# A retention and state space mixer: its state recurrences placed among the projections, its output transposes one chunk later, and the first attention worked by pairs of heads

## The chip, the cores and the metric

The kernel runs on one core of a Trainium2 chip. The core has TensorE (PE, with its weight loads PEld), VectorE (DVE), ScalarE (ACT), GpSimd (POOL) and SyncE (SP, which issues most DMAs). The metric is the device time of one execution in microseconds (us), given as the median of the runs.

## What is computed

The reference is a small network of two blocks. The first takes 512 tokens of width 1024 through a projection, an attention of 8 heads of 64 dimensions that mixes three dilation patterns, a spatial gating, a layer norm and a mixture of 32 experts. The second block treats 512 latent tokens and a context of 256 tokens, in two layers. The first layer mixes by retention and a state space model, the second by latent-compressed attention, each followed by a gated feed-forward part. The mixer of the first layer is what most of this change is about:

```python
def chunked_decay_scan(q, k, v, log_a, s0):
    ...
    scores = jnp.einsum('bhnid,bhnjd->bhnij', qc, kc) * decay
    y_intra = jnp.einsum('bhnij,bhnjv->bhniv', scores, vc)
    ...
    kv_chunk = jnp.einsum('bhnjd,bhnj,bhnjv->bhndv', kc, to_end, vc)
    def step(s, inp):
        kv_n, tot_n = inp
        return tot_n[..., None, None] * s + kv_n, s
    ...
    y_inter = jnp.einsum('bhnid,bhni,bhndv->bhniv', qc, jnp.exp(cum), s_before)
```

It runs forwards and backwards, for 8 retention heads (q, k, v from the projection, q and k of the latents with rotary embedding, a fixed decay per head) and for 8 state space heads (SSD: a convolved input, a decay that depends on the token). The context starts from zero, and the latents start from the context's last states. Then both results are normalised, multiplied by gates, put side by side and multiplied by an output matrix.

## The kernel before

All large products are taken in float32 by splitting each operand into two halves of fp32r, high and low (`split`, L239 and L240: ACT copies the high half `wh`, DVE subtracts for the low half `wl`), and by three matmuls (`mm3`). A projection, `gemm_a`, goes over chunks of 512 output columns; a chunk's weights are four casts of 128x1024, and for each of the token tiles (four for the latents) 24 matmuls of 128x512 into a bank `ga` follow, and an evacuation. A scheduler puts the emitted instructions in order on each engine from the order in which they are written and from what they need; generators with `yield` let two pieces of code be written interleaved.

**First attention** (`block1`). For each head, four score products (queries of tile qt against the keys of tiles 0 to qt, K of 64 rows, into a bank `sc`), on DVE the mask's add, the row maximum, and after ACT's exponential one reciprocal of 128x4 for the head and a multiplication. Then the probabilities `pr` are transposed by PE (`tpb`) and copied to `pt`; at every second head the two heads' value products go to `pvb`, in the two column halves of the array. `fill(FL[3])` steps a filler three times a head: matmuls with one column of weights (`adb`) for the second block's modulation.

**The latent mixer** (`lm`, a class `Mixer` with `proj`, `rope`, `spread`, `states`, `outputs`). The trace has it from 762.5 to 1004.3 us. It is written in this order: the q and k projections with the SSD's time steps among them (`steps`: `smp`, `dt`, a chain of small DVE instructions, `expb`); `rope` of q and of k; the v projection; `spread`, which transposes x, q and k (`mtb`); `states`, which for each of four chunks of 128 tokens forms the retention's products (`kv_ret`: DVE scales v into `vfb`, PE gives `kvr`, DVE and ACT copy it to `SBr`), then for each the SSD's (`kv_ssd`: `btb`, `xsd`, `kvsb`, `SBs`), and then runs the recurrence over the chunks both ways (`carry`: on POOL for the retention, L1240 and L1241, on DVE for the SSD, L1243 and L1244). `outputs` then goes over the chunks n: `inside(n)` (retention scores `ret_s` and `PT`; the SSD's decay matrix `ssd_x` with `Rf` and `Rb` from `mask`, its exponential `E`, `ssd_s`; then the part of the states, `ret_i` with `rint` and `ssd_i` with `sint`), and one chunk behind it `gather(n-1)` (`ret_o` and `ssd_o`, the norms and gates, the result in `res`) and at once `turn(n-1)`, which transposes the result by PE (`ytb`, L1404) into `yT` for the output projection. That projection (`ga` from `yT`) follows, its first weights `wro` being loaded by `early` in the last chunk; then the norm for the next part (`ntb`).

The context's mixer (two chunks) runs the same code, stepped as filler among the experts of the first block.

```python
for n in range(self.nt + 1):
    if n < self.nt:
        o[n] = yield from self.inside(n)
        ...
    if n >= 1:
        self.gather(n - 1, o.pop(n - 1), ynw)
        if self.lat:
            self.turn(n - 1)
```

## Time and profile before

| | us |
|---|---|
| median of 3 runs | 2356.21 (2354.01 to 2359.71) |
| the profiled execution | 2353.49 |
| its span, first to last instruction | 2351.7 |
| PE busy | 2252.5 (96%) |
| DVE busy | 1423.6 (61%) |
| ACT busy | 794.9 (34%) |
| POOL busy | 442.9 (19%) |

A busy share is taken over the whole span, which holds stages with different limits: in the experts (some 300 to 640 us) the DMA engines are the busiest, in most of the rest PE. The mean granted clock of TensorE was 0.977 of full speed. A stage is read from its own stretch of the windows view, where the busy times of all engines and the granted clock stand side by side; what an engine stood idle for is read from the waits.

### The profile page before, as it was taken

How to read it: one execution, taken by the hardware profiler on the slowest of the kernel's cores; microseconds unless marked ns; L12 is line 12 of the kernel's file. 1: busy time of each engine (PE TensorE's matmuls, PEld its weight loads, DVE VectorE, ACT ScalarE, POOL GpSimd, SP SyncE). 2: the span in 40 equal slices, each digit the busy share in tenths (PEclk: the TensorE clock that was granted, in tenths of full speed). 3: DMA queues.
4: the chain of work that ended last, by engine and by line, in shares of the span. 5: the costliest groups of instructions: out<-in, count | busy, mean ns of one | idle time of the engine just before them, and what ended most of it. 6: DMA issues, size and time to landing. Idle time of an engine off the chain costs nothing.

```text
span 2351.7 us, 30149 instructions
## 1 busy us (share of the span) xinstructions
PE 2252.5 (96%) x11748; PEld 1688.6 (72%) x11748; DVE 1423.6 (61%) x2341; ACT 794.9 (34%) x1382; POOL 442.9 (19%) x331
## 2 busy tenths in 40 slices
PE   9999999999979988899999999989999999999998
PEld 7667755534458756688888888877877668888876
DVE  8766743434475577776677753465568765444446
ACT  4344323222253243342211112134446545222222
POOL 0010310232250256410000000531022123000006
PEclk9999999999989997999999999999999999999999
DMA  8655498998853001344344331221100043332230
GB/s 297 217 183 202 182 373 332 371 389 336 310 197 99 30 28 54 125 152 135 122 139 135 126 108 55 65 97 62 60 1 1 1 147 107 106 99 92 87 106 39
DMA packets 99151, 338.91 MB, mean 144 GB/s; under 512 B 14373, under 2 KB 16293, under 8 KB 99002
## 3 DMA queue, kind: packets, MB, share of 16 engines
q1 hardware_dynamic: 94394, 324.33, 39.1%
q0 software_dynamic: 4608, 12.59, 1.5%
q8 instruction: 94, 1.54, 0.3%
q14 instruction: 55, 0.45, 0.1%
HBM read 323.21 MB, written 17.86 MB: 145 GB/s over the span
## 4 chain that ended last, share of the span: by engine, by line
PE 72%; DVE 8%; issue 3%; POOL 2%; ACT 2%; DMA 0%; POOLq 0%; SPq 0%; DVEq 0%; ACTq 0%
PE gb L243 22%; PE ob L243 14%; PE ga L243 10%; PE cb L243 6%; PE gu L243 5%; PE sc L243 3%; PE yb L243 3%; PE ptb L1808 2%; DVE wl L240 1%; POOL rs_r L290 1%; PE kb L243 1%; PE vb L243 1%; PE ntb L920 1%; PE ssd_x L243 1%; PE tpm L687 1%
## 5 line engine op out<-in xcount | busy, mean ns | idle before, releaser
L239 ACT CAST wh<-wr 128x1024 fp32r<-128x1024 f32 (+1 forms) x239 | 249.1, 1048 | 629.1 <-PE gb L243 274.9
L240 DVE TENSOR_TENSOR wl<-wr,wh 128x1024 fp32r<-128x1024 f32 (+1 forms) x235 | 309.2, 1323 | 216.4 <-ACT wh L239 211.8
L243 PE MATMUL gb<-fh,wh 128*128 128x512 f32 x672 | 264.0, 393 | 0.0
L243 PE MATMUL gb<-fh,wl 128*128 128x512 f32 x672 | 263.9, 393 | 0.0
L243 PE MATMUL gb<-fl,wh 128*128 128x512 f32 x672 | 263.7, 392 | 0.0
L243 PE MATMUL ob<-wh,hidh 128*128 128x512 f32 x440 | 173.9, 395 | 4.4 <-DVE gob L1529 3.0
L243 PE MATMUL ob<-wl,hidh 128*128 128x512 f32 x440 | 172.5, 392 | 0.0
L243 PE MATMUL ob<-wh,hidl 128*128 128x512 f32 x440 | 172.3, 392 | 0.0
L1536 DVE TENSOR_TENSOR acc<-acc,ob 128x512 f32<-128x512 f32 x160 | 108.3, 685 | 84.6 <-PE ob L243 84.6
L860 DVE SCALAR_TENSOR_TENSOR adacc<-wr,cond,adacc 128x512 f32<-128x512 f32 x224 | 152.9, 752 | 1.4 <-DMA wr<-in_w_ada 1.4
L243 PEld LDWEIGHTS gb<-fh,wl 128*128 128x128 f32 x672 | 126.2, 188 | 28.7
L243 PEld LDWEIGHTS gb<-fl,wh 128*128 128x128 f32 x672 | 126.2, 188 | 27.7
L243 PEld LDWEIGHTS gb<-fh,wh 128*128 128x128 f32 x672 | 126.2, 188 | 27.4
L243 PE MATMUL gu<-mw,xgT 128*64 128x512 f32 x512 | 124.3, 600 | 0.7 <-issue 0.7
L243 PE MATMUL cb<-fh,wh 128*128 128x256 f32 x416 | 118.0, 284 | 0.0
L243 PE MATMUL cb<-fl,wh 128*128 128x256 f32 x416 | 117.6, 283 | 0.0
L243 PE MATMUL cb<-fh,wl 128*128 128x256 f32 x416 | 117.0, 281 | 0.0
L1538 POOL TENSOR_TENSOR acc<-acc,gate 128x1024 f32<-128x1024 f32 x10 | 28.1, 2811 | 468.1 <-DVE acc L1536 468.1
L290 POOL TENSOR_TENSOR rs_r<-rs_v,mhalf 128x1 f32<-128x1 f32 (+1 forms) x54 | 46.4, 861 | 336.8 <-DVE rs_v L288 336.5
L243 PEld LDWEIGHTS ob<-wh,hidh 128*128 128x128 f32 x440 | 82.6, 188 | 24.8 <-DVE gob L1529 3.2
L1491 DVE TENSOR_TENSOR sg<-sg,gb 128x512 f32<-128x512 f32 x42 | 28.9, 688 | 112.3 <-PE gb L243 112.2
L243 PEld LDWEIGHTS ob<-wh,hidl 128*128 128x128 f32 x440 | 82.7, 188 | 18.3
(666 smaller groups left out, 4891.3 us busy)
## 6 DMA issues: line engine op xcount, KB each, us to landing
mw<-in_w_gu SPq DMA_DIRECT2D x128, 512.0 KB
wr<-in_w_ada SPq DMA_DIRECT2D x96, 512.0 KB
mw<-in_w_dn SPq DMA_DIRECT2D x64, 512.0 KB
wr<-in_w_fg SPq DMA_DIRECT2D x44, 512.0 KB
wr<-in_w_fu SPq DMA_DIRECT2D x44, 512.0 KB
wr<-in_w_fd SPq DMA_DIRECT2D x44, 512.0 KB
wr<-in_w_ret SPq DMA_DIRECT2D x28, 512.0 KB
wr<-in_w_in SPq DMA_DIRECT2D x19, 512.0 KB
```

The costliest lines, as they stand in the source:

```text
L239: self.nc.scalar.copy(h, src)
L240: (eng or self.nc.vector).tensor_tensor(l, src, h.bitcast(F32), ALU.subtract)
L243: self.nc.tensor.matmul(out, lhsT, rhs, start=start, stop=stop, **kw)
L290: nc.gpsimd.tensor_tensor(r, v, self.mhalf[:, :n], ALU.pow)
L687: nc.tensor.transpose(bank[:, k, :], xg[:, (j * 4 + k) * P:(j * 4 + k + 1) * P], self.ident)
L860: V.scalar_tensor_tensor(acc[:, r], W[:, k], s, acc[:, r], op0=ALU.mult, op1=ALU.add)
L920: nc.tensor.transpose(bank[:, j, i * P:i * P + P], hp[i][:, (2 * kk + j) * P:(2 * kk + j + 1) * P], self.ident)
L1491: nc.vector.tensor_tensor(t, t, out[1], ALU.mult)
L1536: V.tensor_tensor(a[:, sl], a[:, sl], ob, ALU.add)
L1538: G.tensor_tensor(a, a, gate(tt), ALU.mult)
L1808: nc.tensor.transpose(bank[:, qt * P:qt * P + P], prs[h][qt][:, kt * P:kt * P + P], K.ident)
```

## The change

The first attention goes by pairs of heads p. For a tile of queries the two heads' score products are written one behind the other (they read the two halves of the rows of `qT` and `kT`), into banks of two tags, from the longest (qt = 3) to the shortest; each tile of queries has its own maximum, sum and reciprocal of 128x1; the odd head's probabilities lie in `res`. The transposes and value products of a pair are written among the scores of the next pair. The filler has the same number of steps as before.

In the mixer, `rope` is done tile by tile in the evacuation of q and k. `states` becomes `states_s` (SSD) and `states_r` (retention). The latents' `spread_x`, `kv_ssd` and SSD recurrence are written among the tiles of the q and k projections, at 1.25 steps a tile; `inside(0)` without `ret_i`, and then the retention's states, among the tiles of the v projection and behind it. `ret_i` moves into `carried(n)`, behind the states; the next chunk's mask is written behind it. The transposes `turn` come one chunk later. The loads of `wro` are written behind `outputs`. The tiles `xsd` and `sts` get large buffers of their own for the latents. The number of matmuls is the same.

```diff
-FL = (0, 1, 1, 3, 1)
+FL = (0, 1, 1, (2, 2, 1, 1), 1)
...
+        def scores(p, qt):
...
+            sc = [ps.tile([P, 512], F32, name="sc", tag=tag, bufs=2) for tag in ("sc", "mm")]
+            for c in range(2):
+                r = slice(64 * c, 64 * c + 64)
+                self.mm(sc[c][:, :n], qT[r, p, qt * P:qt * P + P], kT[r, p, :n], True, True)
+            for c in range(2):
...
+                V.tensor_tensor(pv, sc[c][:, :n], amask[:, 512 - n:], ALU.add)
+                V.tensor_reduce(mx, pv, AX, ALU.max, negate=True)
+                S.activation(pv, pv, AF.Exp, bias=mx, accum_out=ls)
+                V.reciprocal(ls, ls)
+                V.tensor_scalar(pv, pv, ls, None, op0=ALU.mult)
...
+        for p in range(5):
+
+            for i in range(NT):
+                if p < 4:
+                    scores(p, NT - 1 - i)
+                    fill(FL[3][i])
+                if p and i:
+                    spread(p - 1, i - 1)
+                    if i > 1:
+                        values(p - 1, i - 2)
...
+    def carry_s(self, n, d, t_):
...
+        V.tensor_tensor(t_.rearrange("p (g h v) -> p g h v", g=2, v=64), self.SBs(n)[:, :, d, :].rearrange("p g (h v) -> p g h v", v=64), tot, ALU.mult)
+        V.tensor_tensor(to, to, t_.rearrange("p (g c) -> p g c", g=2), ALU.add)
...
-        for n in range(self.nt + 1):
+        for n in range(self.nt + 2):
             if n < self.nt:
                 o[n] = yield from self.inside(n)
-                if n == self.nt - 1 and ahead:
-                    ahead()
                 yield
-            if n >= 1:
+                if self.lat and n == 0:
+                    yield from self.states_r()
+                self.carried(n, o[n])
+                if n + 1 < self.nt:
+                    self.masks[n + 1] = self.mask(n + 1)
+                yield
+            if 1 <= n <= self.nt:
                 self.gather(n - 1, o.pop(n - 1), ynw)
-                if self.lat:
-                    self.turn(n - 1)
+                yield
+            if self.lat and n >= 2:
+                self.turn(n - 2)
                 yield
...
-        steps = lm.steps()
-        for i, _ in enumerate(lm.proj(range(0, 2))):
-            if i % 2 == 0:
-                next(steps, None)
-        lm.rope(lm.q)
-        lm.rope(lm.k)
-        run_gen(lm.proj(range(2, 3)))
-        run_gen(lm.spread())
-        run_gen(lm.states())
...
+        fill = states()
+        interleave(lm.proj(range(2)), fill, LF)
+        run_gen(fill)
+        run_gen(lm.spread_qk())
+        lm.work = k.w4
+        fill = lm.outputs()
+        interleave(lm.proj(range(2, 3)), fill, 1)
+        lm.work = k.work
+        run_gen(fill)
```

How it moves the instructions is seen at three places. A row gives line, operation, what it writes and reads and its shape, and in brackets the queues that it waits for.

The first place is on PE, the start of the first attention, where `sc` are score products and `adb` the filler. Before:

```order
L243 MATMUL sc<-kT,qT 128x128
L243 MATMUL sc<-kT,qT 128x256
L243 MATMUL adb<-wr,cond 32x128
L243 MATMUL sc<-kT,qT 128x384 [waits DVE_49]
L243 MATMUL adb<-wr,cond 32x128 x2
L243 MATMUL sc<-kT,qT 128x512 [waits DVE_49]
L243 MATMUL adb<-wr,cond 32x128 [waits DMAHW4_49]
L243 MATMUL adb<-wr,cond 32x128 x7
L243 MATMUL sc<-kT,qT 128x128 [waits DVE_49]
L243 MATMUL adb<-wr,cond 32x128 [waits DMAHW5_49]
L243 MATMUL adb<-wr,cond 32x128 x4
L243 MATMUL sc<-kT,qT 128x256 [waits DVE_49]
```

Here each head's products follow one another by length, with the filler between. Now:

```order
L243 MATMUL sc<-kT,qT 128x512 x2
L243 MATMUL adb<-wr,cond 32x128 x3
L243 MATMUL sc<-kT,qT 128x384 x2
L243 MATMUL adb<-wr,cond 32x128 [waits DMAHW4_49]
L243 MATMUL adb<-wr,cond 32x128 x7
L243 MATMUL adb<-wr,cond 32x128 [waits DMAHW5_49]
L243 MATMUL adb<-wr,cond 32x128 x7
L243 MATMUL sc<-kT,qT 128x256 [waits DVE_49] x2
L243 MATMUL adb<-wr,cond 32x128 [waits DMAHW6_49]
L243 MATMUL adb<-wr,cond 32x128 x7
L243 MATMUL sc<-kT,qT 128x128 [waits DVE_49] x2
L243 MATMUL adb<-wr,cond 32x128 [waits DMAHW7_49]
```

The first pair's score products stand two and two (x2). Further on the scheduler has put other work between the two of a pair in 7 of the 16 cases; side by side are one pair of 512 columns, three of 384, two of 256 and three of 128.

The second place is on DVE, at the change from the k to the v projection, where the weights of v are cast (`wl`) near the last tiles of k and their rotary steps. Before:

```order
L1144 TENSOR_TENSOR ropew<-k,ropet 128x256
L1146 TENSOR_TENSOR k<-ropew 128x8x32 [waits DVE_49,Pool_49]
L1147 TENSOR_TENSOR k<-ropew 128x8x32 [waits DVE_49]
L240 TENSOR_TENSOR wl<-wr,wh 128x1024 [waits DMAHW0_49,Activation_49]
L240 TENSOR_TENSOR wl<-wr,wh 128x1024 [waits DMAHW1_49,Activation_49]
L240 TENSOR_TENSOR wl<-wr,wh 128x1024 [waits DMAHW2_49,Activation_49]
L1120 TENSOR_SCALAR k<-ga 128x512 [waits PE_49]
L240 TENSOR_TENSOR wl<-wr,wh 128x1024 [waits DMAHW3_49,Activation_49]
```

The casts stand among the rotary steps of k's last tiles. Now:

```order
L1276 TENSOR_TENSOR SBs_6743<-SBs_6743,sts 128x2x256 [waits DVE_49]
L1276 TENSOR_TENSOR SBs_6742<-SBs_6742,sts 128x2x256 [waits DVE_49]
L1275 TENSOR_TENSOR sts<-SBs_6743,latex 128x512 [waits DVE_49]
L1275 TENSOR_TENSOR sts<-SBs_6742,latex 128x512 [waits DVE_49]
L1137 TENSOR_SCALAR k<-ga 128x512 [waits PE_49]
L1276 TENSOR_TENSOR SBs_6743<-SBs_6743,sts 128x2x256 [waits DVE_49]
L1162 TENSOR_TENSOR ropew<-k,ropet 128x256 [waits DVE_49]
L1164 TENSOR_TENSOR ropew<-k,ropet 128x256
L1166 TENSOR_TENSOR k<-ropew 128x8x32 [waits DVE_49,Pool_49]
L1167 TENSOR_TENSOR k<-ropew 128x8x32 [waits DVE_49]
L1276 TENSOR_TENSOR SBs_6742<-SBs_6742,sts 128x2x256
L240 TENSOR_TENSOR wl<-wr,wh 128x1024 [waits DMAHW0_49,Activation_49]
```

The SSD recurrence (`sts`, then `SBs`, twelve instructions of 128x512, of which the last eight are shown) and the last rotary step stand in front of the first cast for v.

The third place is on PE, in the loop over chunks, from the state products of chunk 2 to the output products of chunk 1. Before:

```order
L243 MATMUL ret_i<-SBr,qT 128x128 [waits DVE_49] x2
L243 MATMUL ret_i<-SBr,qT 128x128 x6
L243 MATMUL ssd_i<-SBs_7021,bcT 128x512 [waits Activation_49]
L1404 MATMUL ytb<-c_ident,res 128x128 [waits DVE_49]
L1404 MATMUL ytb<-c_ident,res 128x128 x7
L243 MATMUL ssd_i<-SBs_7021,bcT 128x512 [waits PE_49]
L243 MATMUL ret_o<-v,PT 128x64 [waits Activation_49]
L243 MATMUL ret_o<-v,PT 128x64 x7
L243 MATMUL ssd_o<-xst,E 128x64 [waits DVE_49,PE_49,Pool_49]
L243 MATMUL ssd_o<-xst,E 128x64 x7
```

The transposes `ytb` of chunk 0 stand between chunk 2's state products and the output products of chunk 1. Now:

```order
L243 MATMUL ssd_i<-SBs_6743,bcT 128x512 [waits DVE_49,PE_49]
L243 MATMUL ssd_i<-SBs_6743,bcT 128x512 [waits Activation_49]
L243 MATMUL ret_i<-SBr,qT 128x128 [waits DVE_49]
L243 MATMUL ret_i<-SBr,qT 128x128 [waits Activation_49]
L243 MATMUL ret_i<-SBr,qT 128x128 x6
L243 MATMUL ret_o<-v,PT 128x64 [waits DVE_49]
L243 MATMUL ret_o<-v,PT 128x64 x7
L243 MATMUL ssd_o<-xst,E 128x64 [waits DVE_49,PE_49,Pool_49]
L243 MATMUL ssd_o<-xst,E 128x64 x7
L1464 MATMUL ytb<-c_ident,res 128x128 [waits DVE_49]
L1464 MATMUL ytb<-c_ident,res 128x128 x7
```

The output products of chunk 1 come first, and `ytb` of chunk 0 behind them. In the same loop the first chunk's `ret_i` has moved to the end of the v projection, behind the retention's products:

```order
L243 MATMUL kvr<-vfb,k 128x256 [waits DVE_49,PE_49,Activation_49]
L243 MATMUL kvr<-vfb,k 128x256
L243 MATMUL kvr<-vfb,k 128x256 [waits PE_49,Activation_49]
L243 MATMUL kvr<-vfb,k 128x256
L243 MATMUL ret_i<-SBr,qT 128x128 [waits PE_49,Activation_49,Pool_49]
L243 MATMUL ret_i<-SBr,qT 128x128 [waits PE_49,Activation_49]
L243 MATMUL ret_i<-SBr,qT 128x128 x6
L243 MATMUL ret_s<-qT,kT 128x128 [waits PE_49,Activation_49]
```

`kvr` and the first `ret_i`, which had the SSD's state products and the first chunk's scores between them, are neighbours now. On PE further: between `dt` and `expb` stand 24 matmuls `ga` and 22 transposes, where 48 `ga` stood; and 36 `ga` of the output projection stand ahead of the last chunk's `ytb`, where 62 stood.

## Rows read from the trace of the kernel before

**Rows 1.** The page, costliest groups: line, engine, operation, count; busy, mean; idle.
```profile
L240 DVE TENSOR_TENSOR wl<-wr,wh 128x1024 fp32r<-128x1024 f32 (+1 forms) x235 | 309.2, 1323 | 216.4 <-ACT wh L239 211.8
```

**Rows 2.** Windows: length, busy of PE, PEld, DVE, ACT, POOL; granted clock, DMA share, GB/s.
```profile
86.50:146.50 60.00, 60.00 (x547) 31.84 (x546) 43.61 (x116) 33.22 (x91) 0.00 (x0) 1.00 0.57 192
762.50:835.20 72.70, 71.97 (x341) 56.96 (x341) 39.73 (x78) 16.96 (x22) 14.99 (x18) 1.00 0.08 24
857.00:874.20 17.20, 10.50 (x50) 5.44 (x49) 16.39 (x17) 8.14 (x26) 14.69 (x9) 0.74 0.00 0
886.50:910.70 24.20, 18.10 (x91) 13.76 (x90) 17.76 (x25) 8.02 (x23) 17.37 (x11) 0.70 0.10 34
910.70:937.70 27.00, 21.58 (x122) 17.00 (x121) 19.74 (x29) 10.12 (x21) 14.67 (x8) 0.75 0.18 59
937.70:958.50 20.80, 17.10 (x72) 13.24 (x71) 15.90 (x29) 5.35 (x10) 10.15 (x7) 0.91 0.36 127
958.50:1004.30 45.80, 39.02 (x170) 30.54 (x171) 34.12 (x47) 21.90 (x38) 21.41 (x15) 0.90 0.29 103
```

**Rows 3.** Waits of PE, 762 to 1005 us: total, times, longest.
```profile
PE ytb L1404 <- DVE res L1373: 15.0, 3, 6.1
PE ssd_i L243 <- DVE SBs L1244: 5.0, 1, 5.0
PE ga L243 <- DVE wl L240: 4.3, 5, 1.5
...
PE ret_i L243 <- DVE PT L1286: 1.7, 1, 1.7
```

**Rows 4.** Timeline of PE, first attention: start, duration, records (two to a matmul).
```profile
89.95 0.64 PE L243 MATMUL adb<-wr,cond 128*32 128x128 f32 x16
90.52 0.48 PE L243 MATMUL sc<-kT,qT 64*128 64x128 f32 x2
90.94 0.62 PE L243 MATMUL adb<-wr,cond 128*32 128x128 f32 x10
...
93.33 1.12 PE L243 MATMUL sc<-kT,qT 64*128 64x512 f32 x2
94.38 0.42 PE L243 MATMUL adb<-wr,cond 128*32 128x128 f32 x6
```

**Rows 5.** Timeline of PE from the q projection to the end of v's.
```profile
782.66 0.96 PE L243 MATMUL dt<-c_dtsel,dts 128*128 128x16 f32 x8
...
795.09 0.38 PE L243 MATMUL expb<-latla,c_utri 128*128 128x32 f32 x2 [0.49 <-DVE latla L1094]
...
834.99 0.39 PE L243 MATMUL ga<-wh,al 128*128 128x512 f32 x1
835.22 1.03 PE L1156 MATMUL mtb<-c_ident,xsT 128*128 128x128 f32 x8
836.09 0.60 PE L243 MATMUL kvr<-vfb,k 128*128 128x256 f32 x2
```

**Rows 6.** Timeline of PE, the output product of two chunks.
```profile
884.64 1.95 PE L243 MATMUL ssd_o<-xst,E 128*128 128x64 f32 x16
...
907.13 3.62 PE L243 MATMUL ssd_o<-xst,E 128*128 128x64 f32 x16
```

**Rows 7.** Timeline of DVE: a rotary step, and two steps of the state chain.
```profile
807.56 0.41 DVE L1142 TENSOR_TENSOR ropew<-k,ropet 128x256 f32<-128x256 f32 x1
...
847.79 0.81 DVE L1243 TENSOR_TENSOR stt<-SBs,latex 128x512 f32<-128x512 f32 x1
...
852.21 0.91 DVE L1244 TENSOR_TENSOR SBs<-SBs,stt 128x512 f32<-128x512 f32 x1
```

**Rows 8.** Groups of DVE, 838 to 874 us; columns as rows 1.
```profile
L1244 DVE TENSOR_TENSOR SBs<-SBs,stt 128x512 f32<-128x512 f32 x6 | 9.6, 1611 | 0.1
```

**Rows 9.** Groups of POOL, 838 to 874 us.
```profile
L1241 POOL TENSOR_TENSOR SBr<-SBr,stt 128x256 f32<-128x256 f32 x6 | 7.1, 1196 | 10.5 <-ACT SBr L1209 10.2
...
L1240 POOL TENSOR_TENSOR stt<-SBr,rtot 128x256 f32<-128x256 f32 x4 | 3.1, 780 | 0.3
```

More of the change, by code (lines that the diff above doesn't have):

```diff
@@ L407, in block1, with spread @@
+        def spread(p, jt):
+            o, w = sum((NT - j) * P for j in range(jt)), (NT - jt) * P
+            for c in range(2):
+                if jt == 0:
+                    PTs[p, c] = p1.tile([P, 1280], F32, name="pt", tag="pt", bufs=3)
                 bank = ps.tile([P, 512], F32, name="tpb", tag="tp", bufs=2)
@@ L1217, in kv_ssd @@
         S.copy(bt, bank[:, :256])
[L1218 removed]
+        if not self.lat:
+            xd = self.work("xsd")
+        else:
+            if n % 2 == 0:
+                self.room2 = self.big("xsd")
+            xd = self.room2[:, n % 2 * 1024:n % 2 * 1024 + 1024]
+        xd = xd.rearrange("p (g d h v) -> p g d h v", g=2, d=2, h=4)
         for d in range(2):
@@ new lines, in states_s @@
+    def states_s(self):
+        K, nt = self.K, self.nt
+        if self.lat:
+            self.spread_x()
+            yield
+        st = [self.big(f"SBs{j}") for j in range(2)]
+        hn = nt // 2
+        self.SBs = lambda n: st[n // hn].rearrange("p (t g d c) -> p t g d c", t=hn, g=2, d=2)[:, n % hn]
+        self.ends(((self.SBs(0)[:, :, 0], K.fin_s[:, :, 0]), (self.SBs(nt - 1)[:, :, 1], K.fin_s[:, :, 1])))
+        for n in range(nt):
+            self.kv_ssd(n)
+            yield
+        t = self.big("sts") if self.lat else self.work("sts")
+        for n in range(nt):
+            self.carry_s(n, 0, t[:, 0:512])
+            self.carry_s(nt - 1 - n, 1, t[:, 512:1024])
+        yield
@@ L1945, in scan @@
                 yield
-            yield from cm.spread()
-            yield from cm.states()
+            cm.spread_x()
+            yield
+            yield from cm.spread_qk()
+            yield from cm.states_r()
+            yield from cm.states_s()
             yield from cm.outputs()
```

245 lines of the change are left out of this document (118 added, 127 removed).

## The prediction

> **What bounds the kernel now.** I read the windows view first, stage by stage, then PE's waits in the stages where the granted clock or PE's busy time drops, then the timelines around those waits. In the first attention PE is busy in all 60.00 us, at a full clock, while DVE has 43.61 us of work [rows 2]: this stage is bound by PE, and DVE has 16 us to spare. In the latent mixer it changes in the middle. Up to 835.2 us, the projections, PE has 71.97 of 72.70 us and a full clock. In the four windows shown of the chunk loop, the first chunk and then 886.5 to 958.5 us, PE is busy for 10.50 of 17.20, 18.10 of 24.20, 21.58 of 27.00 and 17.10 of 20.80 us, at a granted clock of 0.70 to 0.91, so that even the busy time is stretched [rows 2, 6]: the output product of one chunk took 1.95 us and that of the next 3.62, which is the step from 2.4 to 1.2 GHz. What PE waits for there is the result of the chunk before (`res`), in front of its transposes: 15.0 us in three waits; then the SSD states, 5.0 us, and `PT`, 1.7 [rows 3]. DVE is busy for 16 to 20 us in each of these windows, POOL for 10 to 17. So the loop is a chain over several engines with PE standing in it, and the sum below is made stage by stage.
>
> **The first attention.** The number of matmuls is the same. A score product of 512 columns takes 1.05 us from its start to the next, one of 128 takes 0.42 [rows 4]; between them I take 0.84 and 0.63 for 384 and 256. If the second of two adjacent products in opposite row halves costs nothing, the nine adjacent pairs give 1.05 + 3 x 0.84 + 2 x 0.63 + 3 x 0.42 = 6.1 us. The trace shows no such pair of scores, so the bounds are 0 and 6.1; I take 6.1, since PE has no idle time here that would hide it. Against it stands the start: the first transposes now wait until the first pair is through DVE, about a quarter of DVE's 43.61 us, at 86.5 + 10.9 = 97.4. Up to there PE has 2.9 us of paired scores, 3.6 of the next pair's, and 51 filler matmuls of two records each at 0.57 us for 16 [rows 4], 3.6 us: 10.1 us, to 96.6. That leaves 0.8 us; I take 2.0, as two casts and key copies lie on DVE there too (bounds 0 and 4). The 24 more reciprocals have DVE's spare time for cover. **Minus 4.1 us.**
>
> A rule speaks against this. The Trainium skill, TensorEngine Tiling (Array Packing), section Performance Considerations, says that tiling speeds up TensorE but not the emptying of PSUM, which may become the bottleneck. Here the emptying engine has 43.61 us of work and PE would keep 53.9, so the rows leave room; by the rule the pairs would give nothing, which is part of a rival below.
>
> **Projections of q, k and v.** Three new waits, each read from the order of instructions and priced by rows. First, `expb` has had 48 `ga` in front of it since `dt` and now has 24 and 22 transposes: 24 x 0.23 + 22 x 0.11 = 7.9 us of cover [rows 5]. The chain behind `dt` took 12.4 us; without the four casts inside it (1.3 each [rows 1], 5.2) and with two rotary steps (four instructions of 0.41 [rows 7], 3.3 for both) it takes 10.5. Wait: 2.6, taken as 2.5 (bounds 0 and 4.5). Second, the casts for v stand behind the SSD recurrence on DVE: 12 x 0.86 (the mean of 0.81 and 0.91 [rows 7]) = 10.3, two rotary steps 3.3, one cast 1.3, together 14.9 us after the last state product; PE's cover is 24 `ga` and 32 transposes, 9.0 us. Wait: 6.0 (bounds 0 and 15). All of PE stands behind that cast, because PE takes its work in order. Third, `ret_i` of the first chunk stands right behind `kvr` and waits for the recurrence on POOL, of which three adds and two multiplications come after the last product: 3 x 1.196 + 2 x 0.780 = 5.1 [rows 9]; taken as 5.0 (bounds 0 and 6). In return the waits for the SSD states (5.0) and for `PT` (1.7) go [rows 3], since the first chunk's scores now lie under v's matmuls; so do the 0.7 us idle before 835.2, and the slow clock from 857 to 874.2, 10.50 x 0.26 = 2.7 us [rows 2]. 13.5 - 10.1: **plus 3.4 us.**
>
> **The chunk loop.** With the transposes of chunk n a chunk later, PE doesn't stand for `res` in front of the next chunk's output products. The 15.0 us of waits go [rows 3], and with them some of the slow clock; what is late next is DVE. Its work in the three windows from 886.5 to 958.5 is 17.76 + 19.74 + 15.90 = 53.4 us of 72.0 [rows 2], and it moves along with the loop. At full clock PE's own work there is 18.10 x 0.70 + 21.58 x 0.75 + 17.10 x 0.91 = 44.4 us, so PE isn't the limit. I take DVE's time as the new length: **minus 18.6 us** (bounds minus 27.6 by PE's work, and minus 9.3, if half of the waits come back as waits for `rint`, `E` or `sint`). This is the term on which the forecast stands.
>
> **The output projection.** 36 instead of 62 matmuls stand ahead of the last transposes, so 26 x 0.23 = **6.0 us** of work that filled the last wait now come behind it. In the last window PE is idle for 6.8 us and runs at 0.90 [rows 2]; of its waits for `wl` (4.3 in all [rows 3]) and the rest I expect some to go, as these matmuls find their weights cast: **minus 4.0 us** (bounds 0 and minus 10.7, all idle time and the slow clock). The loads of `wro` move behind the loop; the 36 matmuls ahead cover theirs, and without that cover it is one more wait of a cast, 1.3 us. The context's steps lie among the experts, where DMA and not PE is the limit; I cost them at nothing.
>
> **Sum.** -4.1 + 3.4 - 18.6 + 6.0 - 4.0 = -17.3 us. Against the profiled execution, 2353.5 us, that is 2336.2; that execution is 2.7 us below the median of the runs, 2356.2, so the median should come to 2338.9. A difference under 0.2% (4.7 us) can't be told from none here.
>
> **Rivals.** *The new waits don't come* (the scheduler's neighbours finish earlier than my rows say): without the 13.5 us the time is 2325.4. For it: DVE is busy for only 39.73 of 72.70 us up to 835.2 [rows 2]. Against: both queues hold the late work in front, in order.
>
> *The pairs give nothing*, because 7 of 16 are separated and the adjacent ones are limited by the emptying of their banks, and the start's wait stays: 6.1 us less, 2345.0. Against: DVE's 16 us to spare.
>
> *Given back.* The chunk loop is a chain of latencies, and only half of its term comes (-9.3); attention and output projection give nothing: 3.4 - 9.3 + 6.0 = +0.1, 2356.3. For it: in the loop neither DVE nor POOL is full (17.76 and 17.37 of 24.20 us [rows 2]).
>
> *Slower: DVE beside POOL in the v projection.* DVE's instructions stretch when POOL is at work: the same 128x512 add that took 0.91 us had a mean of 1.611 in a stretch with POOL on 14.69 of 17.20 us [rows 2, 7, 8]. If the twelve of the recurrence take 1.611, the casts for v come 9.0 us later still. Then the first chunk's DVE work, 16.39 us [rows 2], stands with four casts (5.2) and the scaling of v among v's 96 matmuls (22 us) and exceeds them by some 4.6; and with PE waiting so, the clock falls to the 0.70 of [rows 2], 22 x (1/0.70 - 1) = 9.4. -17.3 + 9.0 + 4.6 + 9.4 = +5.7: 2361.9. It decides where the recurrence's mean passes about 1.4 us and the first cast for v comes over 12 us after PE could use it. The Trainium skill, GPSIMD Engine Reference, section Specifications, states that GpSimd shares its SBUF interfaces with VectorE and contends with instructions of two SBUF inputs, as these are; the rows agree with it in direction. Against this rival: POOL has only 14.99 us of work in the 72.7 us of projections.
>
> **Chances.** Forecast 0.50; no new waits 0.15; no gain from pairs 0.10; given back 0.14; slower 0.11. Faster 0.75, same 0.14, slower 0.11. The range: at the low end no new waits and the largest gain at the output projection, 2325.4 - 6.7, about 2319; at the high end given back, 2356.3 and a little, 2358. The slower case lies outside.
>
> **What would show it.** In the profile of the changed kernel: the waits of `ytb` for `res` under 6 us instead of 15.0; the stretch from the second chunk's scores to the last `ytb` shorter by about 20 us, with DVE busy for over nine tenths of it; new waits of `ga` for `wl` at the start of v near 6 us, of `ret_i` near 5, of `expb` near 2.5; the first attention about 56 us long. I am wrong if the clock in the chunk loop stays at 0.70 to 0.75 with PE waiting elsewhere, or if the wait in front of v grows over 12 us.

## The result, and the profile after

The changed kernel takes 2371.65 us (median of 6 runs, 2368.16 to 2375.93), the kernel before in the same series 2355.11. The ratio is 1.0075, with a 95% interval of 1.0051 to 1.0099: slower by some 16.5 us, where 17.3 us of gain were forecast. The time lies outside the range. The two traces differ by 14.7 us in span (2366.4 against 2351.7), and I cut both at the same landmarks: the first `sc`, the first matmul behind the attention's output projection, the routing's first product and the last `yb` of the experts, and in the mixer `smp`, the second chunk's `ret_s`, the last `ytb` and the first product of the next part.

| stretch | before | after | difference | forecast |
|---|---|---|---|---|
| first attention and its projection | 109.3 | 105.9 | -3.4 | -4.1 |
| experts, with the context beside them | 333.3 | 340.0 | +6.7 | 0 |
| mixer: projections and first chunk | 106.1 | 115.8 | +9.7 | +3.4 |
| mixer: chunk loop | 84.4 | 81.9 | -2.5 | -18.6 |
| mixer: output projection | 45.7 | 50.0 | +4.3 | +2.0 |
| sum | | | +14.8 | -17.3 |

So one term came close, and the other four were all too low. (The forecast read the loop from the third chunk's scores on; from there it took 72.0 us before and takes 68.7 now.) The windows view of the kernel before shows the last three stretches (length, busy time of PE, PEld, DVE, ACT, POOL with counts; granted clock, DMA share, GB/s):

```profile
768.10:874.20 106.10, 97.87 (x470) 72.49 (x469) 72.69 (x129) 35.29 (x82) 40.69 (x37) 0.96 0.08 27
874.20:958.60 84.40, 69.12 (x360) 53.09 (x360) 61.95 (x96) 27.56 (x66) 52.30 (x30) 0.80 0.20 69
958.60:1004.30 45.70, 38.97 (x170) 30.46 (x171) 34.02 (x47) 21.90 (x38) 21.31 (x15) 0.90 0.29 104
```

and of the changed kernel, with the attention's first 56 us ahead, which answer to the first of [rows 2]:

```profile
87.20:143.20 56.00, 55.20 (x542) 26.92 (x542) 44.73 (x143) 32.06 (x89) 0.00 (x0) 1.00 0.61 207
...
772.30:888.10 115.80, 100.98 (x470) 75.76 (x471) 69.04 (x126) 36.63 (x84) 40.70 (x38) 0.93 0.09 32
888.10:970.00 81.90, 66.47 (x335) 49.10 (x333) 59.43 (x98) 26.73 (x64) 45.87 (x26) 0.76 0.16 53
970.00:1020.00 50.00, 44.00 (x198) 34.62 (x198) 35.27 (x48) 22.20 (x39) 25.75 (x16) 0.93 0.31 103
```

Subtract PE's busy time from each length. In the first stretch PE idles for 14.8 us in place of 8.2, and is busy for 3.1 us longer at a lower clock. In the chunk loop it idles for 15.4 us, where it idled for 15.3: nothing has gone but where it stands. DVE is busy for 73% of the loop in both kernels. And the loop handed 6.0 us of matmuls to the output projection: both together went from 130.1 to 131.9 us, where -16.6 was forecast.

The length of the loop in a single trace says less than it seems to. Three kernels of the experiments (`att_only`, `swap_old`, `old_pairs`) have in this loop the same instructions in the same order on PE, DVE and ACT as the kernel before, and took 81.5, 79.1 and 84.4 us for it. In `swap_old`:

```profile
867.13:946.23 79.10, 63.82 (x360) 48.96 (x359) 62.67 (x96) 27.40 (x66) 52.52 (x30) 0.87 0.22 74
```

PE idles for 15.3 us there as in the kernel before; the 5.3 us between the two are a granted clock of 0.87 against 0.80. So the -2.5 us of the table is less than two executions of one loop differ by.

The waits of PE in the mixer, 766 to 1022 us, answer to [rows 3]:

```profile
PE ytb L1464 <- DVE res L1428: 11.2, 3, 4.2
PE ga L243 <- DVE wl L240: 5.5, 2, 4.5
PE ret_i L243 <- POOL SBr L1267: 5.4, 1, 5.4
PE mtb L1188 <- ACT qT L1190: 5.2, 1, 5.2
PE kvsb L243 <- DVE xsd L1248: 1.5, 1, 1.5
...
PE expb L243 <- DVE latla L1111: 0.8, 1, 0.8
```

The three new waits are there: `mtb` in front of v (forecast 6.0, now 5.2), `ret_i` (5.0, now 5.4), `expb` (2.5, now 0.8). But the wait of `ytb` for `res`, which was to fall from 15.0 to under 6, is still 11.2.

What follows a wait is read from the granted clock in steps of 4 us, same view:

```profile
830.00:834.00 4.00, 3.47 (x18) 2.64 (x16) 4.00 (x8) 3.15 (x3) 0.00 (x0) 1.00 0.00 0
834.00:838.00 4.00, 0.00 (x0) 0.00 (x0) 2.71 (x8) 0.00 (x0) 2.44 (x2) 0.68 0.00 0
838.00:842.00 4.00, 3.30 (x15) 3.12 (x16) 2.86 (x4) 2.95 (x7) 0.00 (x0) 0.50 0.03 9
...
882.00:886.00 4.00, 0.00 (x0) 0.00 (x0) 0.07 (x1) 0.37 (x2) 3.60 (x6) 0.65 0.70 253
886.00:890.00 4.00, 3.79 (x33) 3.57 (x33) 1.42 (x4) 0.00 (x0) 0.34 (x2) 0.50 0.00 0
```

Behind each of the two long waits PE works at 0.50, the step from 2.4 to 1.2 GHz. In the kernel before the projections ran at 1.00 throughout [rows 2]. The first of the waits ends with DVE, whose timeline has the recurrence and the last rotary step in one queue, and with a copy on ACT:

```profile
831.56 1.29 DVE L1276 TENSOR_TENSOR SBs<-SBs,sts 128x512 f32<-128x512 f32 x2
832.77 1.29 DVE L1275 TENSOR_TENSOR sts<-SBs,latex 128x512 f32<-128x512 f32 x2
...
837.22 0.42 DVE L1166 TENSOR_TENSOR k<-ropew 128x256 f32<-128x256 f32 x1 [1.29 <-POOL ropew L1165]
837.56 0.42 DVE L1167 TENSOR_TENSOR k<-ropew 128x256 f32<-128x256 f32 x1
837.89 0.68 DVE L1276 TENSOR_TENSOR SBs<-SBs,sts 128x512 f32<-128x512 f32 x1
838.07 1.07 ACT L1190 COPY qT<-mtb 128x512 f32<-128x512 f32 x2 [4.13 <-DVE k L1167]
838.50 2.35 DVE L240 TENSOR_TENSOR wl<-wr,wh 128x1024 fp32r<-128x1024 f32 x2
```

The view names `qT` on ACT for the wait, which PE ends at 838.70. ACT's copy itself waited 4.13 us for the last write to k, at 837.56, the end of the rotary step, which had the recurrence ahead of it and waited 1.29 us for POOL. The casts for v begin at 838.50, and PE doesn't wait for them. So the wait has about the size that was forecast, but it isn't the wait of `ga` for `wl` that the forecast named.

In the experts the groups view (300 to 620 us; busy, mean of one; idle) has one line that moved. Before:

```profile
L243 PE MATMUL gu<-mw,xgT 128*64 128x512 f32 x512 | 124.3, 600 | 0.7 <-issue 0.7
```

After:

```profile
L243 PE MATMUL gu<-mw,xgT 128*64 128x512 f32 x512 | 133.0, 603 | 1.2 <-issue 0.7 <-DVE xgT L705 0.6
```

The same 512 records (256 matmuls), each as long as before, yet 8.7 us more of busy time, and PE doesn't wait. A mean of one instruction says nothing on how far it overlaps with its neighbour.

### The profile page after: what moved, and what is told of

It reads as the page before. It is cut to its first block, busy times and chain, and to the rows that moved or that the text cites. A ratio compares the mean times of both kernels' runs of the same rounds, so it can differ in the third digit from the quotient of the medians.

```text
span 2366.4 us, 30151 instructions
## 1 busy us (share of the span) xinstructions
PE 2262.1 (96%) x11748; PEld 1688.9 (71%) x11748; DVE 1416.2 (60%) x2365; ACT 795.6 (34%) x1382; POOL 438.6 (19%) x331
## 4 chain that ended last, share of the span: by engine, by line
PE 54%; DVE 4%; POOL 2%; issue 2%; ACT 1%; POOLq 0%; ACTq 0%; DVEq 0%
PE gb L243 19%; PE ob L243 14%; PE cb L243 6%; PE ga L243 6%; PE sc L243 3%; PE ptb L1868 2%; DVE wl L240 1%; POOL rs_r L290 1%; PE vb L243 1%; PE kb L243 1%; PE ssd_x L243 1%; PE ntb L937 0%; DVE gob L1589 0%; PE ads L243 0%; DVE ycat L1427 0%
## 5 line engine op out<-in xcount | busy, mean ns | idle before, releaser
L1596 DVE TENSOR_TENSOR acc<-acc,ob 128x512 f32<-128x512 f32 x160 | 108.3, 685 | 84.6 <-PE ob L243 84.6
L243 PE MATMUL gu<-mw,xgT 128*64 128x512 f32 x512 | 133.0, 603 | 1.2 <-issue 0.7
```

Of the source, the lines that this page charges most:

```text
L243: self.nc.tensor.matmul(out, lhsT, rhs, start=start, stop=stop, **kw)
L1596: V.tensor_tensor(a[:, sl], a[:, sl], ob, ALU.add)
```

## The experiments

Six series were run, each beside the kernel before, whose median was 2350.76 to 2354.77. From the second series on every kernel also holds the attention by pairs, `turn_only` too, where its expectation names one edit only; its attention's stretch of 105.9 us in place of 109.3 shows it. In the diffs `Mixer0` is the class before.

### The three parts alone

```diff
  (att_only: the kernel before with the new block1 and FL)
  (ctx_only: the kernel before with)
-        cm = Mixer0(k, "ctx", ...)
+        cm = Mixer(k, "ctx", ...)
  (lat_only: the kernel before with)
-        lm = Mixer0(k, "lat", ...)
+        lm = Mixer(k, "lat", ...)
  (no_ctx: the changed kernel with)
-        cm = Mixer(k, "ctx", ...)
+        cm = Mixer0(k, "ctx", ...)
```

> The kernel before with the attention by pairs alone. Theory: the trace of the change has the projection behind the attention 3.8 us earlier than before, so this alone gives -3.8 us (ratio 0.998). Rival: the attention shifts the arrivals of later weights and costs elsewhere: 0 or more.

> The kernel before with the context's mixer alone in the new order (states of the retention, then of the SSD, ret_i split off, the mask later). Theory: the change's trace lost 7.5 us between 500 and 564 us, where the context's chunks lie among the experts, so this alone costs +7.5 us (ratio 1.003), and the stretch from the first context ret_s to the last expert is as long as in the change. Rival: the experts' stage, bound by DMA, varies from run to run: 0 us.

> The kernel before with the latents' mixer alone in the new order. Theory: +11.5 us (ratio 1.005), all of it from the q projection to the first matmul of the feed-forward part: +9.7 up to the second chunk's ret_s, -2.4 in the chunk loop, +4.2 behind the last transposes. Rival: the latents' stage suffers only together with the other parts (its buffers and queues): under +4 us.

> The change with the context's mixer in the old order. Theory: attention and latents together, -3.8 + 11.5 = +7.7 us against before. Rival (the context costs nothing): the change's own +17 us.

Measured, against 2351.83: `att_only` 2348.11 (0.9978, 0.9963 to 0.9993), `ctx_only` 2359.62 (1.0024, 1.0008 to 1.0039), `lat_only` 2368.11 (1.0065, 1.0040 to 1.0090), `no_ctx` 2365.45 (1.0051, 1.0034 to 1.0067). The attention gains, both others lose, and the parts add up within the noise: -3.7 + 7.8 + 16.3 = 20 against the 16.5 of the whole. `lat_only` and `no_ctx`, with +16.3 and +13.6, lie 5 to 6 us above what was expected; in their traces the mixer's first stretch takes 119.0 and 117.4 us, against 115.8 in the changed kernel. In `ctx_only` the experts' stretch is 341.3 us, in `lat_only` 332.9: that loss belongs to the context's order.

Its trace shows what it is. PE among the experts, where `ssd_x` of the context stands between pieces of `gu` (records, two to a matmul):

```profile
511.34 1.94 PE L243 MATMUL gu<-mw,xgT 128*64 128x512 f32 x8
513.21 1.12 PE L243 MATMUL ssd_x<-Rb,c_ustrict 128*128 128x512 f32 x2
514.26 1.93 PE L243 MATMUL gu<-mw,xgT 128*64 128x512 f32 x6
516.12 1.12 PE L243 MATMUL ssd_x<-Rf,c_m_gt 128*128 128x512 f32 x2
517.18 1.07 PE L243 MATMUL gu<-mw,xgT 128*64 128x512 f32 x2
518.18 1.12 PE L243 MATMUL ssd_x<-Rb,c_ustrict 128*128 128x512 f32 x2
```

From start to start four matmuls take 1.87 us, three 1.86 and a single one 1.00. `gu` uses the two column halves of the array (128*64), one expert in each, and two neighbours in opposite halves cost no more than one. An odd piece has cut a pair, and its loose half costs a full one. The Trainium skill, TensorEngine Tiling (Array Packing), section Key Properties, says that different tiles can work in parallel; the rows agree, and show that the order of the queue decides whether they do. In PE's order `gu` comes in 32 pieces before, 14 of them odd (7 cut pairs), and with the context's new order in 44, 26 odd (13): six more cut pairs at 1 us, of the 8.7.

### The pairs of the experts

```diff
  (ctx_fast: the changed kernel with the latents before, and)
-        interleave(k.moe(p4, psm, ahead, got), fill, 2.25)
+        interleave(k.moe(p4, psm, ahead, got), fill, 3.5)
```

> The attention by pairs and the context in the new order, the latents as before, and the filler among the experts at 3.5 steps instead of 2.25. In the experts the gate and up products (gu, 64 columns of the array each) run two at a time; in the order of instructions the context's matmuls cut them into 44 runs, 26 of odd length, in the change, 32 with 14 odd before, and here 22 with 4 odd. Theory (a pair that is cut apart costs about 1 us): the stretch from the first expert to the last takes 328 us, against 333 before and 341 with the new order, and the total is -8.5 us against before (-3.7 attention, -5). Rival (the new order of the context's steps costs by itself, whatever the pairs): the stretch stays at 341, total +4.

Measured: 2367.45 (1.0068, 1.0046 to 1.0089), experts 353.1 us. A miss. The order had only 4 odd pieces, but the faster filler crowded the front: in windows of this kernel the DMA share from 305 to 400 us is 0.78, where it was 0.92, and what was not loaded there is loaded at the end: in the last 60 us of the experts the share is 1.03, where it is 0.86 in the kernel before. Two things were changed at once, so the run says nothing on pairs.

```diff
  (old_pairs; ctx_pairs and best likewise)
-                    for e in range(2):
-                        self.mm(gu[e * 64:e * 64 + 64, :], ...)
+                    with self.tc.tile_critical():
+                        for e in range(2):
+                            self.mm(gu[e * 64:e * 64 + 64, :], ...)
```

> The attention by pairs and the context part's new order, with the latents' old order; besides, the two matmuls of each column pair of gu are bound together, so that the instruction order can't set another one between them (71 stretches of gu, none with a cut pair, where the context's new order alone had 44, 26 of them cut). Theory A, the new order of the context costs 8 us because it cuts 6 more pairs (26 against 14, about 1 us each): the experts' stretch falls from 341.3 to about 328 (26 cuts gone by 0.5 us each at least), and the time stands at about -7 us against the kernel before (-3.7 of the attention, +8 of the context, -11 of the pairs). Rival B, the new order costs its 8 us in another way (the context's chain, or the stream of weights): the experts' stretch stays near 341 and the time at +4 or more.

> As ctx_pairs, but with the context in its old order: the kernel before with the attention by pairs and with the pairs of gu bound together, nothing else. Theory A: 14 cut pairs go, the experts' stretch falls from 333.3 to about 326, the time to about -10 us against the kernel before; the difference to ctx_pairs is at most 3 us, since neither has a cut pair. Rival B: ctx_pairs stays 8 us behind this kernel, as the context's new order did without the binding. Rival C, the stream of weights sets the experts' length (its queues stand at .99 in the last 60 us): nothing is gained, the time stays at -4.

> Attention by pairs, with its two score matmuls bound together; pairs of gu and of yb bound together; context in the old order; latents in the old order with their output transposes one chunk later. If the parts add up: -4 to -5 of the attention, -6 of the pairs in the experts, -5 of the later transposes, together about -15 us, 2340. If the stream of weights sets the experts' length, the pairs give nothing and it is about -9, 2346.

Measured: 2793.68, 2796.95 and 2965.89 us (ratios 1.1875, 1.1890, 1.2608). A second miss, of the means: in front of bound pairs PE stands for 149.4 us in 56 waits with nothing to wait for that the profile names, as the timeline of `old_pairs` has it for one, so these runs say nothing on pairs either:

```profile
401.51 1.12 PE L243 MATMUL gu<-mw,xgT 128*64 128x512 f32 x2 [6.44 <-issue]
```

The cheap way is to look at why the order cuts a pair. The weights of half 0 are loaded first, so its matmul is free to go while the other half's load is still under way; written in the other order, the first waits for the later load, and both are free together. That this is the reason is argued and not shown by itself; that no odd piece is left is shown:

```diff
  (swap_old: att_only with, and swap_ctx: ctx_only's context, att_only's attention, with)
-                    for e in range(2):
+                    for e in (1, 0):
                         self.mm(gu[e * 64:e * 64 + 64, :], xT[:, c * 2 + k, e * 64:e * 64 + 64], W[e][:, k, :],
```

> The kernel before with the attention by pairs, context and latents in the old order; in the experts the loop over the two column halves of gu runs 1, 0 in place of 0, 1. The half whose weights come last is then first, and the other is free to go with it: in the instruction order 32 stretches of gu, none with an odd number, where the kernel before has 14 odd ones. Theory A, a pair with another matmul between its halves costs 0.5 to 1 us more: 7 cut pairs go, the experts' stretch falls from 333.3 to 326 to 330, the time to about -8 us against the kernel before (-3.7 of the attention). Rival C, the stream of weights sets the experts' length: no gain, -4.

> As swap_old, with the context part in its new order (36 stretches of gu, none odd; without the swap 44, of them 26 odd). Theory A, the context's new order costs 8 us by the pairs that it cuts: no loss is left, the experts' stretch is within 2 us of swap_old's and the time too, about -8 against the kernel before. Rival B, the new order costs by itself: the experts' stretch is 6 to 8 us longer than swap_old's, the time at about 0.

Measured, against 2354.76: `swap_old` 2346.75 (0.9966, 0.9950 to 0.9982), `swap_ctx` 2346.58 (0.9974, 0.9956 to 0.9991), experts 329.0 and 328.7 us. With no pair cut, the new order of the context costs nothing. The groups view of `swap_ctx`:

```profile
L243 PE MATMUL gu<-mw,xgT 128*64 128x512 f32 x512 | 117.7, 601 | 1.6 <-issue 0.7 <-DVE xgT L705 0.5 <-DMA mw<-in_w_gu 0.3
```

13 cut pairs 133.0 us, 7 of them 124.3, none 117.7: 0.9 to 1.5 us for each. Over the other kernels, without `ctx_fast` and those of bound pairs, `gu` is busy for 117.1 to 119.9 us with no pair cut (six traces), 124.3 to 126.7 with 7 (seven) and 133.0 to 134.9 with 13 (three), so this is no matter of one execution; the length of the experts' stretch is less steady, some 332 to 335 us in six of the traces with 7 cut pairs and 338 in that of `turn_only`. PE, not the DMA queues, set the experts' length down to these 329 us: in `swap_old` PE's busy time there fell from 321.2 to 314.1 us, and its idle time grew from 12.1 to 14.9. The .99 in rival C above isn't found in the kernel before, where the DMA share of the last 60 us is 0.86; in `ctx_fast`, where it is 1.03, PE idled for 8.6 of these 60 us.

### The latents' two waits

```diff
  (ret_late: no_ctx with)
                 if self.lat and n == 0:
                     yield from self.states_r()
-                self.carried(n, o[n])
+                else:
+                    if self.lat and n == 1:
+                        self.carried(0, o[0])
+                    self.carried(n, o[n])
  (carry_ret: that, and the recurrence of states_s taken out into carries())
-        fill = lm.outputs()
+        def late():
+            yield from lm.carries()
+            yield from lm.outputs()
+        fill = late()
```

> The change with the context in the old order, and ret_i of the first chunk behind the second chunk's inside instead of right behind kvr. Theory: the wait of ret_i for the recurrence on POOL (5 us) and the stretch at half clock behind it go, -7 us against the same kernel without this (2365 in the last call, so 2358, or +6 against before). Rival: DVE and POOL get to chunk 0 later, the wait moves to ret_o or ytb, 0 us.

> As the last kernel, and the SSD recurrence on DVE behind the casts of v's weights instead of ahead of them. Theory: the wait at the start of v (5.2 us) and the stretch at half clock behind it go, -8 us against the last kernel (2350, or -2 against before); the granted clock is 1.00 from 800 us to the end of v. Rival: the recurrence then holds up the first chunk among v's tiles, and the wait comes back there as PT or ssd_i: 0 us.

Measured, against 2354.59: `ret_late` 2359.33 (1.0031, 1.0011 to 1.0051), `carry_ret` 2351.63 (0.9995, 0.9981 to 1.0009). Both times are as the theory had it: from 13.6 us over the kernel before (`no_ctx`) to 4.7 and then -3.0. In the traces the mixer's first stretch holds 3.7 and 5.4 us of that (117.4, 113.7 and 108.3 us), with PE idle for 14.6, 11.3 and 9.4; the rest lies in stretches that the edits don't touch. In `ret_late` a wait of `kvr` for `vfb` (3.2 us) came for that of `ret_i`. The first stretch of the mixer in `carry_ret`:

```profile
771.10:879.40 108.30, 99.00 (x453) 73.21 (x452) 70.96 (x121) 32.32 (x70) 35.20 (x30) 0.97 0.08 25
```

108.3 us at a clock of 0.97, against 115.8 at 0.93: with the two waits (1.8 us of the first is left, in front of k's transposes) the slow clock went. It still isn't shorter than the 106.1 of the kernel before. What the early states free, they take back in smaller waits (`PT` 2.7, `vfb` 2.4).

### The chunk loop

```diff
  (turn_only: att_only with)
-        for n in range(self.nt + 1):
+        for n in range(self.nt + 2):
...
-                if self.lat:
-                    self.turn(n - 1)
+                yield
+            if self.lat and n >= 2:
+                self.turn(n - 2)
                 yield
```

> The kernel before with the latents' output transposes one chunk later and nothing else. The prediction's term for this: -18.6 in the chunk loop, +6.0 and -4.0 behind it, -16.6 us. Theory now: the loop is a chain through DVE, ACT and POOL (squares on ACT, the power on POOL, then DVE) that takes its time whether PE waits or not, and the waits only change their place: from the second chunk's ret_s to the last ytb 84 us as before, total within 3 us of before.

Measured: 2346.17 (0.9960, 0.9941 to 0.9979); less the attention's 3.7, the later transposes gain 4.7 us, though this interval and that of `att_only` overlap (`swap_turn` and `swap_old`, below, are 5.2 us apart). The loop:

```profile
877.90:956.40 78.50, 66.83 (x359) 52.16 (x358) 64.26 (x96) 27.40 (x66) 49.73 (x28) 0.84 0.20 66
```

Its 78.5 us are hardly less than the 79.1 of `swap_old`, which has the loop of the kernel before; PE's idle time in it fell to 11.7 us, from 15.3 there and 13.2 in `att_only`. PE's waits in the mixer, against [rows 3], are:

```profile
PE ssd_o L243 <- DVE E L1761: 6.9, 1, 6.9
...
PE ytb L1855 <- DVE res L1823: 4.2, 3, 2.9
```

The wait for `res` fell to 4.2, and a wait for `E` of 6.9 came for it. In DVE's queue `E` (905.98 us) stands right behind the result (`res`, 905.38), so what stood behind the result now makes PE wait itself. The timeline of one chunk of the changed kernel shows what holds DVE:

```profile
925.26 0.68 DVE L1408 TENSOR_TENSOR ycat<-ret_o,rint 128x512 f32<-128x512 f32 x1
...
932.03 0.15 DVE L1424 TENSOR_SCALAR frr<-frr 128x1 f32<-128x1 f32 x1 [1.44 <-ACT sq L1422]
...
933.24 2.35 POOL L1354 TENSOR_TENSOR Rf<-Rf,Rb 128x1024 f32<-128x1024 f32 x1 [0.69 <-ACT Rf L1352]
...
933.89 1.72 DVE L288 TENSOR_SCALAR rs_v<-frr 128x9 f32<-128x9 f32 x1
...
935.70 1.81 POOL L290 TENSOR_TENSOR rs_r<-rs_v,mhalf 128x9 f32<-128x9 f32 x1
937.54 0.69 DVE L1427 TENSOR_TENSOR ycat<-ycat,rs_r 128x512 f32<-128x512 f32 x1 [1.34 <-POOL rs_r L290]
...
938.82 0.69 DVE L1428 TENSOR_TENSOR res<-ycat,res 128x512 f32<-128x512 f32 x1
...
939.56 1.54 PE L1464 MATMUL ytb<-c_ident,res 128*128 128x128 f32 x6 [3.80 <-DVE res L1428]
```

From DVE's first step on the output product to its transposes the result needs 14.3 us, over DVE, ACT for the squares, POOL for the power -1/2 of 9 numbers, and DVE again. POOL starts the power after a long addition of another chunk. Here the power's input `rs_v`, itself 1.72 us long beside that addition, is ready no sooner (935.61); a chunk earlier it was ready at 913.14, and POOL did the addition first, until 915.5. DVE's waits in the loop of the changed kernel begin with this step:

```profile
DVE ycat L1427 <- POOL rs_r L290: 7.5, 4, 3.0
```

In the kernel before it was 7.8. Two runs take this one step off POOL, in the changed kernel and in the best version so far:

```diff
-        rs = K.rstd(rr, pool, 9, 1.0 / 64, 1e-6)
+        if self.lat:
+            V.tensor_scalar(rr, rr, 1.0 / 64, 1e-6, op0=ALU.mult, op1=ALU.add)
+            V.reciprocal(rr, rr)
+            rs = rr
+        else:
+            rs = K.rstd(rr, pool, 9, 1.0 / 64, 1e-6)
```

> The changed kernel, but the latents' gather takes 1/x on DVE in place of the power -1/2 on POOL (the root is left out). Theory, the loop is a chain of latencies through DVE, ACT and POOL: DVE's waits for rs_r (7.5 us) go, the loop from the second chunk's scores to the last transposes falls from 81.9 to 74 to 77, the time by 4 to 8 us against the changed kernel, which stood at +16.5 against the kernel before: so +8 to +13. Rival, DVE's busy time or PE's clock sets the loop: it stays at 81 to 83, the time at +16.

> swap_turn with the same step off POOL (the root left out). Theory: its waits for rs_r of 6.2 us go, the loop falls from 78.6 to 72 to 75, the time from about -13.5 against the kernel before to -17 to -20. Rival: the loop stays at 78 to 79.5 and the time at -13.

Measured, against 2354.41: `after_recip` 2365.49 (1.0048, 1.0031 to 1.0065), loop 74.7 us in place of 81.9; `turn_recip` (four runs) 2325.45 (0.9877, 0.9856 to 0.9899), loop 71.2 in place of 78.6. The two loops:

```profile
895.30:970.00 74.70, 65.78 (x340) 48.25 (x337) 62.69 (x104) 26.94 (x64) 39.51 (x22) 0.78 0.15 54
866.60:937.80 71.20, 66.75 (x366) 52.23 (x366) 64.48 (x103) 27.25 (x66) 43.35 (x24) 0.87 0.22 74
```

PE's idle time in them, which differed less between executions of one loop (13.2 to 15.3 us) than the length did (79.1 to 84.4), fell from 15.4 to 8.9 us and from 11.6 to 4.5, by about the waits for `rs_r` (7.5 and 6.2), although DVE has a little more work; in `after_recip` `ytb` waits 3.3 us for `res`, not 11.2. The loop is a chain, and DVE's busy time was not its floor. `turn_recip` gained more than was expected, 15.8 us on `swap_turn`. In the traces, 14.2 us apart, the loop and an output projection of 41.2 us in place of 44.1 hold 10.3 of it; the rest lies in stretches that the edit doesn't touch.

### Versions that beat both kernels

```diff
  (swap_turn: turn_only with e in (1, 0) for gu and yb)
  (mend_all: the changed kernel with the edits of carry_ret, and e in (1, 0) for gu and yb)
  (turn_sqrt: turn_recip with)
-            rs = rr
+            rs = pool.tile([P, 9], F32, name="rs_a", tag="rs_a", bufs=2)
+            S.activation(rs, rr, AF.Sqrt)
```

> Attention by pairs; context in the old order; halves of gu and of yb in the order 1, 0; latents in the old order with the output transposes one chunk later. If the parts add up: -3.7 of the attention, -4 of the pairs, -5 of the later transposes, about -13 us, 2342. If the pairs give nothing: -8.4 as turn_only.

> The whole change, with three places mended: the first chunk's carried part behind the second chunk's inside, the SSD recurrence behind v's casts (both as in carry_ret), halves of gu and yb in the order 1, 0. If the two waits with their slow clock and the cut pairs are the whole loss: carry_ret stood at about -1, which had the context in its old order and 14 odd stretches; with none the experts give 3 to 6 more, -4 to -7, about 2346. If the context's new order costs by itself, +4 or more.

> turn_recip with the root of 1/x taken by ACT, so the result is that of the reference again. Eight table loads of 1.28 us come to ACT, which is busy for 27 of 71 us in the loop. If they lie in ACT's idle time, the loop takes 72 to 74 us (71.2 in turn_recip, 78.6 in swap_turn) and the time is about -24 against the kernel before, 2330. If they stand in the chain (two a chunk, 2.6 us, three chunks), the loop goes back to 77 to 80 and the time to -13.

Measured: `swap_turn` 2341.57 (0.9941, 0.9920 to 0.9962) and `mend_all` 2351.61 (0.9980, 0.9965 to 0.9996) against 2354.76, the first as expected, the second a little short of it; `turn_sqrt` 2329.77 (0.9890, 0.9865 to 0.9915) against 2354.77, the best: 25 us under the kernel before and 42 under the changed one. Its loop takes 71.4 us with the root back in. The loop, and the timeline of one chunk:

```profile
869.06:940.47 71.41, 63.62 (x365) 47.11 (x365) 59.96 (x103) 32.28 (x73) 44.16 (x25) 0.92 0.22 73
...
889.36 0.20 DVE L1828 RECIPROCAL frr<-frr 128x9 f32<-128x9 f32 x1
889.65 1.28 ACT L1830 ACT_TABLE_LOAD   x1
890.95 0.21 ACT L1830 ACTIVATE rs_a<-frr 128x9 f32<-128x9 f32 x1
891.29 0.67 DVE L1834 TENSOR_TENSOR ycat<-ycat,rs_a 128x512 f32<-128x512 f32 x1
```

Even with a table load in front, the root is there 1.6 us behind the reciprocal's end; ACT was free for it after 0.1 us, where POOL had its additions first. The loop has only three such loads, two for roots and one for the exponential between; behind the last exponential the last two roots need none. The root isn't free, though: PE idles for 7.8 us in this loop and for 4.5 in that of `turn_recip`, and the length is the same only because the granted clock was 0.92 in place of 0.87. The Trainium skill, ScalarE: Activation LUTs, section What ACT_TABLE_LOAD costs, gives some 1283 ns for a load and 2.66 us for a switch of tables with a drain. The load agrees, 1.28 us here; the drain doesn't show: from the end of the activation before (889.64) to the root (890.95) it is 1.3 us.

## Why the prediction was wrong

**The first attention** came close: -3.4 us in the trace for -4.1. The start's wait is nearly missing (0.5 us in all for 2.0), which leaves some 3.9 us for the pairs in place of 6.1. Two errors, of 1.5 and 2.2 us, thus mostly cancel, so the closeness is partly luck; no run parts the pairs from the start.

**The projections.** The idle time was sized well: forecast at +6.1 us, it came to +6.6. In part this is luck: `expb` waits 0.8 us and not 2.5, small waits that were not forecast make up for it (`kvsb` 1.5, `kvr` 1.3), and the wait in front of v stands at another instruction. The step that failed is the clock: the sum credited 2.7 us for a slow stretch that would go, and charged nothing for those that new waits make. Behind the 5.2 and the 5.4 us PE ran at 0.50, so busy time grew by 3.1 instead of falling by 2.7. That the waits carry the clock's loss with them is shown by `carry_ret`, whose busy time in this stretch is 99.0 us in place of 101.0.

**The chunk loop** holds most of the error, 16 of 32 us. The step that failed was "I take DVE's time as the new length". DVE had the same 26 to 27% of idle time in the loop before, waiting for others, and the sum dropped it with PE's wait, although nothing in the change shortened what DVE waits for. The rows for it were there: the rival "given back", which called the loop a chain of latencies, read from them that neither DVE nor POOL is full. What was measured in place of -18.6 is a loop with PE idle for 15.4 us, as before, at a clock of 0.76, and a chain in which one step, the root on POOL, was worth 6.5 to 7.1 us of that idle time. Alone, the later transposes are worth some 5 us in the whole kernel.

**The output projection.** The 6.0 us of matmuls moved behind the loop came (busy +5.0), the 4.0 us of gain did not: idle time went from 6.7 to 6.0. The step that failed is "I expect some to go": the waits for `wl` were 4.3 us and are 5.5. The longest, 4.5 us, ends with a cast of 1.67 us that starts at 989.92, and whose weights POOL had multiplied by the gate until 988.60. That product is late because the gate is. The gate's load before, the load now, and POOL's wait for it now:

```profile
949.17 0.42 SPq L192 DMA_DIRECT2D gate<-md  x1
971.48 0.84 SPq L192 DMA_DIRECT2D gate<-md  x1
977.91 2.40 POOL L909 TENSOR_TENSOR gate<-gate,gateb 128x1024 f32<-128x1024 f32 x1 [8.91 <-DMA gate<-md]
```

The kernel before issued the gate's load 9.4 us ahead of the last `ytb` (958.55), the changed one 1.5 us behind it (970.00), and POOL waited 8.91 us for it; the forecast asked only for the loads of `wro`. No run takes this load alone, so how much of the 4.0 us it cost is open. The next cast took 3.40 us beside POOL's product of 3.36. The Trainium skill's rule that the prediction weighed, that GpSimd contends with VectorE (GPSIMD Engine Reference, Specifications), agrees with these rows: the same cast took 1.22 us elsewhere.

**The context**, "DMA and not PE is the limit; I cost them at nothing", cost 6.7 us. The windows view of the kernel before has for the experts:

```profile
300.00:640.00 340.00, 330.49 (x1598) 162.85 (x1591) 140.17 (x246) 98.01 (x173) 73.01 (x56) 0.98 0.93 353
```

PE was busy for 330.5 of 340.0 us there, at a DMA share of 0.93. So PE was the busiest, not the DMA engines, as the text ahead of the prediction has it, and PE was the one to ask. The order of `gu`'s pieces held the six more cut pairs.

**The rivals.** Slower was right in sign, but 10 us short (2361.9), and by another way: the recurrence took 0.65 us an instruction (1.29 for two), not 1.611; from 830 to 834 us POOL had no work beside it. What it had right is that a wait at v brings the slow clock.

## What to carry to other kernels

Before a wait is traded for another, follow the chain to the instruction that ends it: if the loop turns over several engines in order, no engine's busy time is its floor, and one small step on a queue with long work (9 numbers behind a 2.35 us addition) can be worth more than moving 32 transposes. Compare a stretch in two traces by idle time and granted clock, not by its length alone. Charge a new wait on PE with the slow clock behind it, as after those of 5.2 and 5.4 us here, not only with its length. And where matmuls are written as pairs on opposite halves of the array, look at the order for odd pieces: here turning a loop of two round was worth 4 us.

## What the runs showed of the hardware

- Two matmuls of 128x512 in opposite column halves cost 0.94 us as neighbours (1.87 for two pairs); a loose one costs 1.00. The mean of a record, 600 ns, is the same in both cases.
- PE's clock stood at 0.50 behind waits of 5.2 and 5.4 us, and reached 0.97 to 0.99 in the slices after that.
- The same loop, instruction for instruction, took 84.4 us at a mean granted clock of 0.80 and 79.1 us at 0.87, with PE idle for 15.3 us both times.
- DVE's `rs_v` on 128x9 took 1.72 us beside POOL's addition of 128x1024, and 0.17 us in the last chunk: even an instruction of 9 columns stretches.
